# Second tile of the context's value sums: column-group matmuls by token in place of 128 multiply-adds on VectorE

## The chip, the cores and the metric

One core of a Trainium2 chip runs the whole program in one launch. The metric is the device time of one execution in microseconds; the median of several executions is compared. Engines are named as in the profile: PE is TensorE, DVE is VectorE, ACT is ScalarE, POOL is GpSimd and SP is SyncE, which issues most transfers.

## The reference, cut to what matters

The program is a transformer block with an MLP, then two layers of a second kind on 256 tokens `x`, beside a context `ctx` of 256 tokens which only the first of these layers updates. Each of them ends in an expert layer (`peer_ffn`): a token has 8 heads, each picks 16 of 16384 experts, so a token has 128 picks; `u` and `v` are rows of 1024 numbers.

```python
def chunk(hc):                      # 128 tokens
    ...                             # eid, gate: 128 tokens x 8 heads x 16 picks
    u = jnp.take(u_tab, eid, axis=0)
    act = jax.nn.gelu(jnp.einsum('chkd,cd->chk', u, hc)) * gate
    v = jnp.take(v_tab, eid, axis=0)
    return jnp.einsum('chk,chkd->cd', act, v)
```

The case is about the last line for the context: each token's output is the sum of its 128 rows of `v`, each times its own `act`. Everything is float32; the context's new state feeds the keys and values of the second layer's attention (`mla_kv`), and nothing else.

## The kernel before

**Two chains.** The main chain computes `x`: block 1, its MLP, then for each of the two layers a mixer and an expert layer in a dense form (every expert is multiplied for all tokens, and the gates are zero where it wasn't picked). Beside it runs the context's chain, `context` (L1502) and `context_peer` (L1514), as a Python generator: after each step of the main chain (one weight tile of 128x1024), `alongside` (L240) advances it by so many steps as the table `PACE` (L28) says for that stage. In the stage `out0` that is one step for each weight tile. A gather waits for the main chain's last weight tile (`behind`, L273), so the pace holds on the chip too. A scheduler then fixes each engine's order when the program is built.

**The main chain in `out0`** (`dense`, L1399, first expert layer): for each pair j of 128-expert columns, `scores` (L1387) makes 2 x 8 x 3 matmuls of 256 columns into `ps`, and `outputs` (L1418) 2 x 4 x 3 matmuls of 512 columns into `acc`. The factor 3 is `mm3` (L375, its three matmuls are L378 to L380): a float32 product is made from a high and a low half of each factor, `wh` by ACT (L363) and `wl` by DVE (L372) for every weight tile. `Gq` times the scores (`da`, L1412) and its halves `dh`, `dl` (L522, L523) are made once for each j. 64 j, four weight tiles each.

**After it** comes `mix1`, the second layer's mixer: first `add_tokens` (L1482) and the norm (L490 to L499), then projections of `w_in`, a convolution on DVE (L917), and its attention, which can't be started before the context's keys are ready (the word "keys" in `run`, L1606).

**The context's sums.** Tokens are in two tiles of 128. For a tile, `gather_acts` (L1225) gathers the rows of `u` and makes `act`, 128 tokens x 128 picks, and `gather_sum` (L1241) gathers the rows of `v`. Both use `fetch` (L1218): one indirect DMA of POOL's queue (L1220) brings 128 rows (512 KB) into one of the four buffers `ug`. The table `VSUM` (L41) chooses a form of the sum for each tile:

- 1, the second tile's: gather number k brings the k-th pick of all 128 tokens, one row for each partition (`eidi`); DVE multiplies it by that pick's `act`, a scalar for each partition, and adds it to `htok` (L1253; the first, L1251, only multiplies). At the end eight 128x128 transposes go through `gacc`, and eight DVE instructions (L1263) add them to the context.
- 0, the first tile's: a gather brings the 128 picks of one token (`eidT`, transposed on TensorE). TensorE sums over the partitions with the token's `act` as weights, so that one column of weights gives one token's sum. `Z` (tile `gz`, L1276) holds such columns spread over 32 columns, zero but for the token's own, and 32 tokens accumulate into 32 rows of PSUM. Two tokens (e) and two halves of the row (n) use four column groups of the array:

```python
for e in range(2):
    for n in range(2):
        c = 64 * n + 32 * e
        mul = nc.tensor.matmul(ga[c:c + 32, :], Z[:, e, m, :],
                               vt[e][0][:, n * 512:n * 512 + 512], start=(mm == 0),
                               stop=(mm == 31), skip_group_check=True, tile_position=(0, c))
        if e == 0:
            self.after(mul, vt[1][1])
```

The last two lines make the first of the four wait for both gathers. `ga` is the only buffer `gacc` of the context's chain. After 64 tokens (a half, q) ACT copies `ga` out (L1295), four transposes and eight DVE instructions (L1303) add it to the context, and `gacc` serves the second half. After the second tile's sum `keys_tile` (L931) makes the second half of the context's keys.

Of the kernel before, what the change touches and what calls it, by code (L numbers as in the profile page):

```python
# [37 lines left out]
TC = 16  # L38
GI = 8
VLOW = False  # L40
VSUM = (0, 1)  # L41
SHARE = ((0.24, 1.32), (0.24, 0.5))
MTS = (2, 2, 2)
DENSE = (2, 5)
# [152 lines left out]
class Net:  # L197
# [1043 lines left out]
    def gather_sum(self, s, x, gcol, tt, acc):  # L1241
# [3 lines left out]
        act = self.acts[tt]  # L1245
        if VSUM[tt]:
            ht = acc()
# [395 lines left out]
```

## Time and profile before

| | us |
|---|---|
| median of 3 runs | 3347.62 (3332.73 to 3351.87) |
| the profiled execution | 3326.9 |
| its span, first to last instruction | 3325.2 |
| TensorE busy in the span | 2956.7 (89%) |
| VectorE busy | 2472.0 (74%) |
| ScalarE busy | 1404.2 (42%) |
| GpSimd busy | 810.8 (24%) |

The profile is of one execution and gives each instruction its start, its length and the line that made it. Matmuls run pipelined, so their recorded lengths overlap: the time that one costs in a row of them is the distance between two starts. A matmul in full float32, such as L1288, leaves two records. "Idle before" is the time for which an engine stood still ahead of an instruction, with what ended it. The granted clock is a share of TensorE's full 2.4 GHz.

In the span, the first tile's sum runs from 969 to 1361 us, beside the first layer's mixer and routing. The second tile's runs from 1840 to 2302 us: beside `out0` until about 2165 us, and then beside the head of `mix1`.

### The profile page before, as it was taken

How to read it: one execution, taken by the hardware profiler on the slowest of the kernel's cores; microseconds unless marked ns; L12 is line 12 of the kernel's file. 1: busy time of each engine (PE TensorE's matmuls, PEld its weight loads, DVE VectorE, ACT ScalarE, POOL GpSimd, SP SyncE). 2: the span in 40 equal slices, each digit the busy share in tenths (PEclk: the TensorE clock that was granted, in tenths of full speed). 3: DMA queues.
4: the chain of work that ended last, by engine and by line, in shares of the span. 5: the costliest groups of instructions: out<-in, count | busy, mean ns of one | idle time of the engine just before them, and what ended most of it. 6: DMA issues, size and time to landing. Idle time of an engine off the chain costs nothing.

```text
span 3325.2 us, 52753 instructions
## 1 busy us (share of the span) xinstructions
PE 2956.7 (89%) x19879; PEld 2530.5 (76%) x19879; DVE 2472.0 (74%) x5129; ACT 1404.2 (42%) x1936; POOL 810.8 (24%) x565
## 2 busy tenths in 40 slices
PE   6989997888799899559999999988889899999998
PEld 4777786777676677348888888876669899888998
DVE  2645559999896579889888888968757998655555
ACT  2444553333334334234445444443434454544443
POOL 0000000444443234405442444511004433000000
PEclk9999988999799989669999999989989999999999
DMA  7777633899987579879998899966444489766664
GB/s 249 250 256 236 209 132 121 277 327 332 345 305 259 199 269 315 297 230 387 362 373 311 331 357 377 363 233 223 140 140 133 147 249 298 263 193 192 211 214 153
DMA packets 289327, 852.87 MB, mean 256 GB/s; under 512 B 25264, under 2 KB 91568, under 8 KB 284592
## 3 DMA queue, kind: packets, MB, share of 16 engines
q1 hardware_dynamic: 147888, 543.16, 47.8%
q0 software_dynamic: 73728, 268.47, 22.1%
q10 hardware_dynamic: 67456, 37.88, 3.8%
q8 instruction: 156, 2.56, 0.3%
q14 instruction: 99, 0.81, 0.1%
HBM read 814.80 MB, written 34.60 MB: 255 GB/s over the span
## 4 chain that ended last, share of the span: by engine, by line
PE 54%; DVE 18%; DMA 14%; issue 8%; ACT 3%; POOL 2%; SPq 0%; DVEq 0%; ACTq 0%; POOLq 0%
PE acc L379 7%; PE acc L380 6%; PE ps L380 6%; PE acc L378 6%; PE ps L378 6%; PE ps L379 6%; DVE wl L372 4%; DMA ug<-in_v_dram,eidT 3%; DMA w<-in_w_in_dram 3%; DMA ug<-in_u_dram,eidi 3%; DVE A L1373 2%; DVE ohB L1370 2%; DVE gz L1233 2%; DMA ug<-in_v_dram,eidi 2%; DMA w<-in_w_mod_dram 2%
## 5 line engine op out<-in xcount | busy, mean ns | idle before, releaser
L363 ACT ACTIVATE wh<-w 128x1024 fp32r<-128x1024 f32 (+1 forms) x818 | 850.5, 1045 | 1013.0 <-PE ps L379 276.3
L372 DVE TENSOR_TENSOR wl<-w,wh 128x1024 fp32r<-128x1024 f32 (+1 forms) x770 | 930.3, 1209 | 452.7 <-PE ps L380 114.8
L380 PE MATMUL ps<-hh,wl 128*128 128x256 f32 x2432 | 702.9, 290 | 30.4 <-DVE wl L372 30.2
L378 PE MATMUL ps<-hh,wh 128*128 128x256 f32 x2432 | 698.6, 288 | 26.8 <-ACT wh L363 14.6
L379 PE MATMUL ps<-hl,wh 128*128 128x256 f32 x2432 | 695.2, 286 | 3.0 <-DVE hl L523 2.9
L1220 POOL DMA_INDIRECT ug<-in_u_dram,eidi x256 | 346.8, 1355 | 1026.6 <-DVE rstd L479 562.5
L378 PEld LDWEIGHTS ps<-hh,wh 128*128 128x128 f32 x2432 | 470.5, 194 | 55.5 <-ACT wh L363 20.3
L380 PEld LDWEIGHTS ps<-hh,wl 128*128 128x128 f32 x2432 | 469.8, 193 | 56.1 <-DVE wl L372 42.4
L379 PEld LDWEIGHTS ps<-hl,wh 128*128 128x128 f32 x2432 | 470.3, 193 | 11.9 <-DVE hl L523 4.6
L379 PE MATMUL acc<-wl,dh 128*128 128x512 f32 x1024 | 407.2, 398 | 12.6 <-DVE wl L372 12.5
L378 PE MATMUL acc<-wh,dh 128*128 128x512 f32 x1024 | 403.4, 394 | 15.9 <-ACT dh L522 12.2
L380 PE MATMUL acc<-wh,dl 128*128 128x512 f32 x1024 | 400.8, 391 | 0.5 <-DVE dl L523 0.5
L1233 DVE SCALAR_TENSOR_TENSOR gz<-ug,htok 128x1024 bf16<-128x1024 f32 x256 | 310.5, 1219 | 22.3 <-DMA ug<-in_u_dram,eidi 22.0
L380 PE MATMUL pre<-hh,wl 128*128 128x256 f32 x896 | 261.8, 296 | 18.7 <-DVE wl L372 10.4
L1220 POOL DMA_INDIRECT ug<-in_v_dram,eidi x128 | 188.4, 1472 | 310.7 <-ACT wh L363 205.6
L379 PE MATMUL pre<-hl,wh 128*128 128x256 f32 x896 | 255.3, 287 | 0.0
L378 PE MATMUL pre<-hh,wh 128*128 128x256 f32 x896 | 254.8, 286 | 0.1
L379 PEld LDWEIGHTS acc<-wl,dh 128*128 128x128 f32 x1024 | 193.5, 189 | 63.4 <-DVE wl L372 28.0
L378 PEld LDWEIGHTS acc<-wh,dh 128*128 128x128 f32 x1024 | 193.6, 189 | 58.8 <-ACT dh L522 12.4
L372 POOL TENSOR_TENSOR wl<-w,wh 128x1024 fp32r<-128x1024 f32 x48 | 131.1, 2732 | 392.7 <-ACT wh L363 192.2
L380 PEld LDWEIGHTS acc<-wh,dl 128*128 128x128 f32 x1024 | 193.5, 189 | 39.8 <-DVE dl L523 1.2
L1220 POOL DMA_INDIRECT ug<-in_v_dram,eidT x128 | 143.2, 1118 | 258.8 <-PE gacc L1288 118.9
(510 smaller groups left out, 5108.1 us busy)
## 6 DMA issues: line engine op xcount, KB each, us to landing
w<-in_uT_dram SPq DMA_DIRECT2D x256, 512.0 KB, 4.6
w<-in_v_dram SPq DMA_DIRECT2D x256, 512.0 KB, 4.4
w<-in_w_in_dram SPq DMA_DIRECT2D x142, 512.0 KB, 4.6
w<-in_w_mod_dram SPq DMA_DIRECT2D x96, 512.0 KB, 4.9
w<-in_w_ff_dram SPq DMA_DIRECT2D x64, 512.0 KB, 5.9
G<-Gs ACTq DMA_DIRECT2D x32, 1024.0 KB, 7.3
Gq<-G SPq DMA_DIRECT2D x32, 1024.0 KB, 7.3
w<-in_w_ada_dram SPq DMA_DIRECT2D x48, 512.0 KB, 4.6
```

Of the source, the lines that this page charges most:

```text
L363: self.step = nc.scalar.activation(hi[:, :n], w[:, :n], AF.Copy)
L372: eng.tensor_tensor(lo[:, :n], w[:, :n], hi[:, :n].bitcast(F32), op=OP.subtract)
L378: mm(out, a[0], b[0], start=start, stop=False, skip_group_check=True)
L379: mm(out, a[0], b[1], start=False, stop=False, skip_group_check=True)
L380: mm(out, a[1], b[0], start=False, stop=stop, skip_group_check=True)
L1220: f = self.nc.gpsimd.indirect_dma_start(out=t, out_offset=None, in_=tab, in_offset=bass.IndirectOffsetOnAxis(ap=idx, axis=0))
L1233: nc.vector.scalar_tensor_tensor(j, ut, 1.0, ht, op0=OP.mult, op1=OP.mult, accum_out=sc[:, k:k + 1])
L1370: nc.vector.tensor_tensor(ohB, iov, over(iT[:, 1, ts]), op=OP.is_equal)
L1373: nc.vector.tensor_tensor(A2[:, i], ohA, over(gp[:, i, ts]), op=OP.mult)
```

## The change

One number in a table: the second tile's sum takes the first tile's form.

```diff
-VSUM = (0, 1)
+VSUM = (0, 0)
```

So for tokens 128 to 255 of the context L1251 to L1264 fall away, and L1266 to L1304 run, with 128 gathers by `eidT` where there were 128 by `eidi`, 256 matmuls L1288 in 64 groups of four, 16 products L1276, and the ends of two halves. The generator takes the same number of steps. What the engines' orders become is seen at four places.

DVE in the middle of `out0`, before: `wl` is the low half of a weight tile, `htok` the sum, `ug` a gathered tile, `da` and `dl` belong to the scores of a j.

```order
L372 TENSOR_TENSOR wl<-w,wh 128x1024
L1253 SCALAR_TENSOR_TENSOR htok<-ug,act,htok 128x1024
L1412 TENSOR_TENSOR da<-da,Gq 128x512
L372 TENSOR_TENSOR wl<-w,wh 128x1024
L1253 SCALAR_TENSOR_TENSOR htok<-ug,act,htok 128x1024
L523 TENSOR_TENSOR dl<-da,dh 128x512
L372 TENSOR_TENSOR wl<-w,wh 128x1024
L1253 SCALAR_TENSOR_TENSOR htok<-ug,act,htok 128x1024
L372 TENSOR_TENSOR wl<-w,wh 128x1024
L1253 SCALAR_TENSOR_TENSOR htok<-ug,act,htok 128x1024
```

DVE at the same place, of the change:

```order
L372 TENSOR_TENSOR wl<-w,wh 128x1024 x3
L1276 TENSOR_TENSOR gz<-eye_80,actT 128x256 x2
L1412 TENSOR_TENSOR da<-da,Gq 128x512
L523 TENSOR_TENSOR dl<-da,dh 128x512
L372 TENSOR_TENSOR wl<-w,wh 128x1024 x4
L1412 TENSOR_TENSOR da<-da,Gq 128x512
```

Where each `wl` had a multiply-add behind it, the `wl` now follow each other, with two products for `Z` every eight groups.

PE in the middle of `out0`, of the change: `acc` belongs to the outputs, `ps` to the scores, `gacc` to the context's sum.

```order
L378 MATMUL acc<-wh,dh 128x512
L379 MATMUL acc<-wl,dh 128x512
L380 MATMUL acc<-wh,dl 128x512
L1288 MATMUL gacc<-ug,gz 32x512 x4
L380 MATMUL ps<-hh,wl 128x256
L378 MATMUL ps<-hh,wh 128x256
L379 MATMUL ps<-hl,wh 128x256
```

In between the matmuls of the main chain stands a group of four; before, there was none here. From the start of the sum to the end of `out0` there are 53 such groups, two for each j; 11 more follow. From a group to the group after next, which uses its two buffers, TensorE mostly has four weight tiles of the main chain to do, at some places three or two. Behind `out0` the weight tile that releases a group's second gather stands at most two tiles ahead of the group.

PE at the end of `out0` and in the norm of `mix1`, before: `dout` is the output of the expert layer on its way back, the L490 sum the squares, L499 spreads the inverse root.

```order
L380 MATMUL acc<-wh,dl 128x512
L539 MATMUL ps<-cst,dout 128x128 x16
L490 MATMUL ps<-ones_74,mt 128x1 x8
L434 MATMUL pg<-w,ca_82 32x512 x4
L490 MATMUL ps<-ones_74,mt 128x1 x8
L499 MATMUL ps<-mt,ones_74 128x256
```

PE at the same place, of the change:

```order
L380 MATMUL acc<-wh,dl 128x512
L1288 MATMUL gacc<-ug,gz 32x512 x4
L539 MATMUL ps<-cst,dout 128x128 x8
L434 MATMUL pg<-w,ca_82 32x512 x4
L539 MATMUL ps<-cst,dout 128x128 x8
L1288 MATMUL gacc<-ug,gz 32x512 x4
L490 MATMUL ps<-ones_74,mt 128x1 x16
L1288 MATMUL gacc<-ug,gz 32x512 x4
L499 MATMUL ps<-mt,ones_74 128x256
```

Three groups have moved into this stretch, two of them in front of steps of the norm.

POOL, before, with all gathers of the program:

```order
L1220 DMA ug<-in_u_dram,eidi 128x1024 x128
L1220 DMA ug<-in_v_dram,eidT 128x1024 x128
L1220 DMA ug<-in_u_dram,eidi 128x1024 x128
L1220 DMA ug<-in_v_dram,eidi 128x1024 x128
L372 TENSOR_TENSOR wl<-w,wh 128x1024 x48
```

POOL, of the change:

```order
L1220 DMA ug<-in_u_dram,eidi 128x1024 x128
L1220 DMA ug<-in_v_dram,eidT 128x1024 x128
L1220 DMA ug<-in_u_dram,eidi 128x1024 x128
L1220 DMA ug<-in_v_dram,eidT 128x1024 x128
L372 TENSOR_TENSOR wl<-w,wh 128x1024 x48
```

Only the list of row numbers of the last 128 gathers is another.

## Rows read from the trace of the kernel before

**Rows 1.** Page, part 1: engine, busy us (share of the span), number of instructions

```profile
PE 2956.7 (89%) x19879; PEld 2530.5 (76%) x19879; DVE 2472.0 (74%) x5129; ACT 1404.2 (42%) x1936; POOL 810.8 (24%) x565
```

**Rows 2.** Stretch, its us; PE, PEld, DVE, ACT, POOL busy; granted clock; DMA share; GB/s

```profile
1843.00:2165.00 322.00, 309.54 (x1905) 273.24 (x1904) 286.35 (x294) 135.76 (x160) 158.87 (x105) 0.99 0.97 362
2165.00:2200.00 35.00, 24.01 (x134) 20.04 (x134) 23.55 (x64) 15.20 (x25) 2.67 (x3) 0.71 0.45 155
2200.00:2310.00 110.00, 97.22 (x705) 84.93 (x704) 88.80 (x176) 39.51 (x60) 22.24 (x18) 0.94 0.79 274
```

**Rows 3.** PE's waits, 1843 to 2165 us: for whom, us, times, longest; then to 2310

```profile
PE ps L380 <- DVE wl L372: 5.7, 5, 3.1
PE acc L379 <- DVE wl L372: 4.8, 3, 1.6
...
PE ps L380 <- DVE wl L372: 11.6, 10, 3.6
```

**Rows 4.** Timeline of PE in out0: start, length, operation

```profile
1910.13 0.28 PE L378 MATMUL ps<-hh,wh 128*128 128x256 f32 x1
...
1912.30 0.40 PE L378 MATMUL acc<-wh,dh 128*128 128x512 f32 x1
...
1916.86 0.39 PE L380 MATMUL acc<-wh,dl 128*128 128x512 f32 x1
```

**Rows 5.** Groups by line, 1850 to 2150 us: busy, mean ns, idle before and releasers

```profile
L1220 POOL DMA_INDIRECT ug<-in_v_dram,eidi x98 | 149.4, 1524 | 151.2 <-ACT wh L363 66.9 <-DVE htok L1253 38.7 <-DVE dl L523 19.6
L1253 DVE SCALAR_TENSOR_TENSOR htok<-ug,act,htok 128x1024 f32<-128x1024 f32 x97 | 124.1, 1280 | 10.2 <-DMA ug<-in_v_dram,eidi 10.2
...
L1412 DVE TENSOR_TENSOR da<-da,Gq 128x512 f32<-128x512 f32 x25 | 17.3, 690 | 14.6 <-ACT da L1397 14.5
```

**Rows 6.** DVE's groups, 1843 to 2310 us; then L1253's busy time in out0

```profile
L1253 DVE SCALAR_TENSOR_TENSOR htok<-ug,act,htok 128x1024 f32<-128x1024 f32 x127 | 162.5, 1279 | 27.6 <-DMA ug<-in_v_dram,eidi 27.5
L917 DVE SCALAR_TENSOR_TENSOR cacc<-up,cols,cacc 128x256 f32<-128x256 f32 x60 | 28.0, 480 | 0.0
...
1843.00:2165.00 322.00, 133.08 (x104) 0.99 0.97 362
```

**Rows 7.** Timeline of DVE in the norm at the head of mix1

```profile
2178.70 1.28 DVE L1253 SCALAR_TENSOR_TENSOR htok<-ug,act,htok 128x1024 f32<-128x1024 f32 x1 [1.09 <-DMA ug<-in_v_dram,eidi]
2181.34 0.16 DVE L493 TENSOR_SCALAR rstd<-ps 128x2 f32<-128x2 f32 x1 [1.36 <-PE ps L490]
```

**Rows 8.** Timeline of PE in the first tile's sum, full clock

```profile
1264.82 0.28 PE L380 MATMUL pre<-hh,wl 128*128 128x256 f32 x1
1265.03 1.07 PE L1288 MATMUL gacc<-ug,gz 128*32 128x512 f32 x8
1266.02 0.38 PE L380 MATMUL pre<-hh,wl 128*128 128x256 f32 x1
1266.24 0.28 PE L378 MATMUL pre<-hh,wh 128*128 128x256 f32 x1
```

**Rows 9.** A group after a wait, and the clock of its stretch (columns as rows 2)

```profile
1252.81 1.93 PE L1288 MATMUL gacc<-ug,gz 128*32 128x512 f32 x8 [2.55 <-DMA ug<-in_v_dram,eidT]
...
1252.80:1255.50 2.70, 2.69 (x12) 1.04 (x13) 2.18 (x16) 0.00 (x0) 0.50 (x1) 0.50 1.02 393
```

**Rows 10.** The small operations: durations in ns, minimum, median, maximum

```profile
L1276 DVE TENSOR_TENSOR gz<-eye,actT x16: 400/422/428, 968.4 to 1273.3; 128x256 f32<-128x256 bf16 x16
L1303 DVE SCALAR_TENSOR_TENSOR cT<-gacc,mod_b_mod,cT x16: 273/275/279, 1173.6 to 1364.3; 128x64 f32<-128x64 f32 x16
```

**Rows 11.** DMA issues, 1850 to 2150 us: count, median us from issue to landing

```profile
ug<-in_v_dram,eidi POOLq DMA_INDIRECT x98, 7.4
```

**Rows 12.** The first tile, 950 to 1352 us: PE's wait, POOL's group, landing

```profile
PE gacc L1288 <- DMA ug<-in_v_dram,eidT: 21.5, 17, 2.9
...
L1220 POOL DMA_INDIRECT ug<-in_v_dram,eidT x126 | 141.3, 1121 | 258.2 <-PE gacc L1288 118.9 <-ACT wh L363 67.1 <-issue 28.5
...
ug<-in_v_dram,eidT POOLq DMA_INDIRECT x126, 5.9
```

## The prediction

> **What bounds the kernel now.** I began with the page's busy line [rows 1]: TensorE is busy 89% of the span and VectorE 74%, an average over stages. The sum that changes runs from 1840 to 2302 us, so I asked for the busy time by stretch [rows 2]: 1843 to 2165 us (the gated sums of the first expert layer, "out0"), 2165 to 2200 us (the norm at the head of the second mixer) and 2200 to 2310 us (that mixer, "mix1"). In out0 TensorE is busy 309.5 of 322 us at a granted clock of 0.99, VectorE 286.4, and the DMA engines are at 97%. All three are near full, so the waits decide [rows 3]: of TensorE's 12.4 idle us in out0, 5.7 and 4.8 us ended with VectorE's low half of a weight tile (wl), the rest with ScalarE's high half (wh), none with a gather. TensorE bounds out0, and VectorE costs it little.
>
> How full that is shows in the starts of matmuls [rows 4]: from 1910.13 to 1912.30 us are 18 starts of 256 columns, 0.12 us each, and from there to 1916.86 us 20 starts of 512, 0.228 us each. A pair of expert columns (one j) has 48 of the first kind and 24 of the second: 48 x 0.12 + 24 x 0.228 = 11.2 us. By the row of L1412, the 25 j of 1850 to 2150 us [rows 5] took 300 / 25 = 12.0 us each. So 0.8 us in 12 are idle or hidden gaps, and nothing large that is added to TensorE fits into them.
>
> **What the change takes away.** VectorE loses one multiplication and 127 multiply-adds of 128x1024, 162.5 us, 133.1 of them in out0 and so 29.4 after it [rows 6]. None of it is directly on TensorE's path. What TensorE felt of it is the waits for wl, 5.7 + 4.8 in out0 and 11.6 - 5.7 = 5.9 after it, 16.4 us in all [rows 3]. A VectorE that has 133 of its 286 us less in out0 should come to nearly all of them in time: **-16.4 us**. Bounds: 0, if the late wl come from late weight tiles, and -28 if out0's hidden gaps go too (0.8 x 27 = 22 us there, 5.9 after). In the norm at 2178 us a multiply-add stands ahead of the first step of the inverse root (L493), but that step then still waited 1.36 us for TensorE [rows 7]: to drop it gives nothing there.
>
> **What it adds.** The 128 gathers, their queue on POOL and their pacing stay; they take their row numbers from the transposed list (order of POOL, in the section on the change). New are 64 groups of four matmuls, one for each two gathered tokens, on the engine that bounds. The first tile shows the price [rows 8]: a matmul of 256 columns starts at 1264.82, the group at 1265.03, and the next two at 1266.02 and 1266.24. From 1264.82 to 1266.24 are 1.42 us where two starts take 0.24 without it, so a group costs 1.18 us: 64 x 1.18 = **+75.5 us**. By the order of TensorE 53 groups stand in out0 (62.5 us) and 11 behind it (13 us). Of the 1.18 us, 0.09 lie ahead of the group and 0.10 behind it. The Trainium skill (TensorEngine Tiling (Array Packing), Key Properties) says that a change of tiling mode drains TensorE; by that rule these 0.19 us are the drain, which each group pays that stands alone, and the trace agrees that there is such a step. Without it the groups would cost 64 x 0.99 = 63 us, with it 75.5. Where the granted clock was 0.50 (1.2 GHz), right after TensorE had waited 2.55 us, a group took 1.93 us [rows 9]; that touches the groups in the norm, where the clock is 0.71 [rows 2], and adds some 2 us there, which I leave out. Could the groups hide? In out0 there are 12.4 us of idle time, and they belong to the waits just counted; in the norm and mix1 11.0 and 12.8 us [rows 2], scattered. So +75.5 stays, with +60 as its lower bound (11 groups hidden whole).
>
> Small additions: 16 products that spread the weights, 0.42 us each on VectorE (6.7 us); a transpose and copy of the activations; for each half of 64 tokens a copy, four transposes and eight short multiply-adds of 0.28 us [rows 10], where now eight of twice the columns end the sum. VectorE has room for all (133 us are freed), and the tail behind the last gather is as long as before within 2 us: 0.
>
> **The new wait.** Now a late gather holds VectorE, 27.5 us in all [rows 6]; afterwards it holds TensorE's queue, with all matmuls of the main path behind it. A group needs two gathers, and four buffers hold two groups; so a buffer comes free with a group, and the group after next uses it. In out0's order mostly four weight tiles stand between these, 4 x 2.8 = 11.2 us plus one group; against it stand two issues on POOL of 1.52 us and a landing of 7.4 us [rows 11], 10.4 us. That fits barely, and some groups stand only two or three tiles apart (5.6 to 8.3 us). The first tile, with the same buffers and the same groups, had 17 such waits, 21.5 us [rows 12], at a landing of 5.9 us and beside emptier DMA queues. Bounds: 0 (every gather in time) and +96 (1.5 us at each of 64 groups: the 10.4 us against three tiles and half a group). I take **+11**, between 0 and the first tile's 21.5, since TensorE's own slower pace (11.2 + 2 x 1.18 = 13.6 us for a j, not 12.0) spreads the same bytes over more time. The matmuls queued behind belong to the main path, and nobody else gets in between.
>
> **Sum:** -16.4 + 75.5 + 11 = +70 us. The profiled execution took 3326.9 us, so it would be 3397; the median of the three runs is 20.7 us above the profiled one, and the measured time is such a median: 3347.6 + 70 = **3418 us**.
>
> **The rivals.**
> *Gathers block TensorE.* If the round trip in out0 is longer than the tiles between a group and its refill, every group waits. For it: landings of 7.4 us in a stage at 97% DMA share, and mix1, where a gather's release stands only one or two tiles ahead of its group in the order. A long wait also brings the lower clock [rows 9]. Against it: VectorE waited only 10.2 us for 97 gathers of out0 [rows 5]. Half of the upper bound, +48 in place of +11: about 3455 us, up to 3503.
> *Gathers come sooner.* POOL's issue of a gather takes 1.52 us in out0 beside multiply-adds on VectorE, 1.12 us in the first tile's stretch [rows 5, 12]. If VectorE's work is what stretches it, two issues get 0.8 us shorter and the new waits vanish, while out0's hidden gaps go as well: 75.5 - 28 = +47, 3395 us. The Trainium skill (SBUF — State Buffer, Who interferes with whom) says that VectorE and GpSimd share a port pair which one instruction holds whole, and that VectorE instructions with two SBUF inputs contend with GpSimd's reads; by that rule this case is the likelier one, though the same section infers that writing descriptors needs only the write side. No run here separates the two yet.
> *No change.* The groups fall where TensorE would idle anyway. All 36 us of idle time in the three stretches of [rows 2] hold 36 of the 75.5; and mix1 ends sooner by the 28.0 us of its convolution on VectorE [rows 6], which starts earlier: +11.5, about 3359 us. The order speaks against it, since 53 groups stand where 12.4 us are idle.
> *Faster.* VectorE, not TensorE, paces out0: it is 89% busy, and TensorE's ends are modelled, so TensorE's busy share could flatter it. Then the 12.0 us of a j are VectorE's, and without 5.1 us of multiply-adds (four for a j) a j falls back to TensorE's 11.2 us plus what of two groups (2.4 us) does not overlap. It decides from the point where less than 0.8 us of these 2.4 lengthen a j; with a sixth (0.4 us) 12.0 becomes 11.6, over 27 j -11 us, and mix1's 12.8 idle us [rows 2] with its lighter VectorE make it -24: about 3324 us. Against it stand the 10.5 us of waits for wl in out0, far too few for an engine that sets the pace.
>
> **How the numbers follow.** Chances: forecast 0.58, gathers block 0.16, gathers sooner 0.14, no change 0.08, faster 0.04. All but the last two are slower. About 0.5%, 17 us, is what a measurement of this kernel can tell from no change: faster 0.04, same 0.08, slower 0.88. The range leaves out the fastest and most of the unchanged cases below (from +17, 3365 us) and above it ends within the upper half of the blocking case (+117, 3465 us).
>
> **What would show it right or wrong.** Right: in the profile after, out0 is about 55 us longer with TensorE still above 95% busy, a j takes some 13.7 us, the row of the group matmuls doubles its count, VectorE's busy time falls by about 155 us, and the waits of TensorE for wl shrink below 5 us. The new waits stand in TensorE's waits as "gacc <- DMA ug"; near 30 us in total (the first tile's 21.5 among them) they fit, near 70 the blocking rival holds. POOL's mean issue in out0 tells the third case: 1.5 us or near 1.0. The prediction is wrong if out0 gets no longer, which says that TensorE had room I did not see, or if a group of four costs clearly other than 1.18 us between 256- and 512-column matmuls.

## The result

| | median us | range | ratio to before, 95% interval |
|---|---|---|---|
| before, 6 runs | 3344.93 | 3332.73 to 3351.87 | |
| changed, 6 runs | 3364.61 | 3363.36 to 3369.87 | 1.0074 (1.0055 to 1.0093) |

The change makes the kernel slower by 0.74%, some 25 us (the two medians alone lie 20 us apart); the forecast was +70. The profiled execution of the changed kernel took 3363.4 us, its span is 3361.7.

Page, part 1, to be read against [rows 1]: TensorE gained 53 us and VectorE lost 137. The durations of VectorE's instructions fell by the 155 us that were worked out; its busy time fell by less, because recorded durations overlap in places.

```profile
PE 3010.0 (90%) x20392; PEld 2537.0 (75%) x20392; DVE 2335.3 (69%) x5026; ACT 1409.6 (42%) x1938; POOL 757.1 (23%) x565
```

Busy time by stretch, the stages of [rows 2] at their new places: out0, the norm, mix1 until the last group.

```profile
1839.00:2208.00 369.00, 364.55 (x2328) 282.53 (x2327) 177.27 (x215) 141.68 (x162) 107.53 (x104) 0.99 0.89 316
2208.00:2243.00 35.00, 28.73 (x196) 22.29 (x195) 20.01 (x61) 16.49 (x27) 4.70 (x5) 0.85 0.52 189
2243.00:2345.00 102.00, 97.61 (x751) 78.88 (x749) 74.94 (x208) 37.37 (x60) 19.18 (x16) 1.00 0.78 281
```

In out0 TensorE is now busy 364.55 of 369 us, and the DMA share fell from 0.97 to 0.89. In the norm and in mix1 TensorE has a higher granted clock than before, 0.85 against 0.71 and 1.00 against 0.94.

TensorE's waits in out0, and then from 2208 to 2345 us (for whom, us, times, longest), to be read against [rows 3]: the waits for wl are gone but for 0.4 us, the waits for gathers that came are 10.6 us.

```profile
PE gacc L1288 <- DMA ug<-in_v_dram,eidT: 4.5, 2, 2.6
...
PE gacc L1288 <- DMA ug<-in_v_dram,eidT: 6.1, 5, 1.8
...
PE ps L380 <- DVE wl L372: 0.4, 1, 0.4
```

A group in out0, in TensorE's timeline (start, length, operation): from 2000.70 to 2002.13 are 1.43 us where two starts take 0.24, so a group costs 1.19 us, as in the first tile [rows 8].

```profile
2000.70 0.28 PE L378 MATMUL ps<-hh,wh 128*128 128x256 f32 x1
2000.91 1.06 PE L1288 MATMUL gacc<-ug,gz 128*32 128x512 f32 x8
2001.91 0.38 PE L379 MATMUL ps<-hl,wh 128*128 128x256 f32 x1
2002.13 0.28 PE L380 MATMUL ps<-hh,wl 128*128 128x256 f32 x1
```

Groups by line, 1850 to 2200 us (busy, mean ns, idle before), against [rows 5]: POOL's issue of a gather takes 1.04 us, not 1.52.

```profile
L1220 POOL DMA_INDIRECT ug<-in_v_dram,eidT x100 | 103.8, 1038 | 252.0 <-PE gacc L1288 102.3 <-ACT wh L363 85.4 <-PE acc L380 19.1
L1288 PE MATMUL gacc<-ug,gz 128*32 128x512 f32 x408 | 54.4, 607 | 4.5 <-DMA ug<-in_v_dram,eidT 4.5
L1412 DVE TENSOR_TENSOR da<-da,Gq 128x512 f32<-128x512 f32 x25 | 17.3, 694 | 3.0 <-ACT da L1397 2.9
```

So price and number of the groups, the vanished waits and the new ones are all as forecast, and yet the profiled span grew by 36.5 us and the time by about 25. By the starts of marked instructions in the two traces: out0 (from the first L1412 on a `da` to the first L1488) is 47 us longer; the norm (to the first L378 of mix1) 3.3 us shorter, 19.4 in place of 22.7; mix1 (to the last L1063) 6.0 shorter, 182.5 in place of 188.5. The rest, ahead of out0 and behind mix1, is -4.2 and +3.1 us; behind mix1 two executions of one kernel differ by as much (next section). In out0 62.5 for its groups and 4.5 of new waits, less the 10.5 of vanished ones, were to give +56.5; behind it 13 + 6.1 - 5.9 were to give +13. So some 10 us are missing in out0, and 22 behind it.

### The profile page after: what moved, and what is told of

Read it like the earlier page. It is cut to its first block, busy times and chain, and to the rows that moved or that the text cites. A ratio compares the mean times of both kernels' runs of the same rounds, so it can differ in the third digit from the quotient of the medians.

```text
span 3361.7 us, 53689 instructions
## 1 busy us (share of the span) xinstructions
PE 3010.0 (90%) x20392; PEld 2537.0 (75%) x20392; DVE 2335.3 (69%) x5026; ACT 1409.6 (42%) x1938; POOL 757.1 (23%) x565
## 4 chain that ended last, share of the span: by engine, by line
PE 61%; DVE 16%; DMA 13%; issue 5%; ACT 3%; POOL 1%; SPq 0%; DVEq 0%; ACTq 0%; POOLq 0%
PE ps L380 7%; PE ps L378 7%; PE acc L379 7%; PE ps L379 7%; PE acc L380 7%; PE acc L378 7%; DMA ug<-in_v_dram,eidT 4%; DVE wl L372 3%; PE gacc L1288 3%; DMA ug<-in_u_dram,eidi 2%; DMA w<-in_w_in_dram 2%; DVE A L1373 2%; DVE ohB L1370 2%; DMA w<-in_w_mod_dram 2%; DVE gz L1233 2%
## 5 line engine op out<-in xcount | busy, mean ns | idle before, releaser
L378 PE MATMUL ps<-hh,wh 128*128 128x256 f32 x2432 | 700.4, 288 | 23.2 <-ACT wh L363 8.9
L378 PEld LDWEIGHTS ps<-hh,wh 128*128 128x128 f32 x2432 | 470.1, 193 | 65.4 <-issue 25.1
L1220 POOL DMA_INDIRECT ug<-in_v_dram,eidT x256 | 281.4, 1099 | 661.1 <-ACT wh L363 294.5
L378 PE MATMUL acc<-wh,dh 128*128 128x512 f32 x1024 | 402.5, 393 | 14.1 <-ACT dh L522 12.2
L1233 DVE SCALAR_TENSOR_TENSOR gz<-ug,htok 128x1024 bf16<-128x1024 f32 x256 | 310.4, 1218 | 19.4 <-DMA ug<-in_u_dram,eidi 19.2
L378 PE MATMUL pre<-hh,wh 128*128 128x256 f32 x896 | 255.4, 287 | 0.1
L378 PEld LDWEIGHTS acc<-wh,dh 128*128 128x128 f32 x1024 | 193.6, 189 | 57.0 <-ACT dh L522 12.5
L380 PEld LDWEIGHTS pre<-hh,wl 128*128 128x128 f32 x896 | 173.4, 195 | 38.4 <-DVE wl L372 15.0
```

What stands on the lines that cost most here:

```text
L378: mm(out, a[0], b[0], start=start, stop=False, skip_group_check=True)
L380: mm(out, a[1], b[0], start=False, stop=stop, skip_group_check=True)
L1220: f = self.nc.gpsimd.indirect_dma_start(out=t, out_offset=None, in_=tab, in_offset=bass.IndirectOffsetOnAxis(ap=idx, axis=0))
L1233: nc.vector.scalar_tensor_tensor(j, ut, 1.0, ht, op0=OP.mult, op1=OP.mult, accum_out=sc[:, k:k + 1])
```

## The experiments

Ratios are to the kernel before in runs beside each; times "x us above" are made from ratios, at 3340 us for the kernel before, whose medians there were 3336 to 3342. A ratio's interval is about 0.2% to either side, 7 us.

### The kernel before, once more

> The kernel before, unchanged, for a second profile. Its six times so far lie between 3332.7 and 3351.9 us, its one profile was of an execution of 3326.9 us, while the six times of the changed kernel lie within 6.5 us of each other. Theory A (the spread belongs to the multiply-adds on VectorE, which TensorE feels in some executions more than in others): the times spread over 15 to 25 us again, and a profile of a slower execution has its extra time in out0 and mix1, between 1840 and 2380 us. Rival: the spread lies elsewhere in the program, and the stretch from 1840 to 2380 us has the same length as in the first profile within 3 us.

Twelve times lie between 3333.6 and 3347.1 us (ratio 1.0002), and the second profile has a span of 3333.1 us, 7.9 above the first: 3.5 us of it in out0, 0.5 in the norm and mix1, 3.6 behind them. Neither theory holds: the difference is spread out, and the kernel without multiply-adds (below) spreads over 14 us too. What follows is smaller: my base, the median of three at 3347.6 us, was 5 to 11 us higher than every later median, and the profiled execution that carried the sum (3326.9 us) was quicker than every timed one of this kernel.

### What the multiply-adds cost by themselves

```diff
-                    nc.vector.scalar_tensor_tensor(ht, vt, act[:, k:k + 1], ht, op0=OP.mult, op1=OP.add)
+                    nc.vector.scalar_tensor_tensor(ht[:, 0:8], vt[:, 0:8], act[:, k:k + 1], ht[:, 0:8], op0=OP.mult, op1=OP.add)
```

> The kernel before, in which the 127 multiply-adds of the second tile read and write 8 of the 1024 columns only, so that the sums of the other columns are left out; the gathers, their order and their release by VectorE stay. It measures what the multiply-adds cost TensorE, by themselves. Theory A (they cost far more than the waits for wl that I counted: hidden gaps between matmuls in out0 and late steps in the norm and mix1 too): 35 to 55 us below the median of before, near 3300 us; out0 (sum's start to first dout) 16 to 22 us shorter than in the profile of before, norm and mix1 another 15 to 19. Theory B (the relief is the 16.4 us of waits for wl as forecast, and the groups cost less than 1.18 us each because part of them falls into idle time): 16 us below, near 3330. In both, POOL's mean issue of a gather falls to about 1.0 us if VectorE's work stretches it, and stays near 1.5 if it belongs to the kind of gather.

3316.8 us, ratio 0.9923 (0.9906 to 0.9940): 26 us below before, between the theories. POOL's issue stays at 1.43 us in out0. Out0 is 11 us shorter, mix1 3, and TensorE still waits for wl: 4.4 us in out0 and 9.6 behind it, though VectorE has next to nothing to do for the sum.

### Gathers that nothing reads

```diff
-                    nc.vector.scalar_tensor_tensor(ht, vt, act[:, k:k + 1], ht, op0=OP.mult, op1=OP.add)
+                    pass
```

> The kernel before, in which the second tile's 127 multiply-adds are left out whole, so that its sum is left out and nothing waits for a gather but the next gather into the same buffer. With e1_no_sum (3316.8 us), where VectorE still reads 8 columns of each gathered tile and so waits for it, this tells apart why TensorE still waited for wl there (4.4 us in out0, 9.6 in the norm and mix1). Theory A (a late gather holds VectorE, and the low halves queued behind it come late): those waits go, 8 to 14 us below e1_no_sum, 3303 to 3309. Theory B (the weight tiles themselves come late, with the DMA engines at 99% in out0): the waits stay, within 4 us of e1_no_sum.

3304.4 us, ratio 0.9891 (0.9868 to 0.9914), 11 us below the run just shown: theory A. TensorE's waits for wl in the norm and mix1, with 8 columns read:

```profile
PE ps L380 <- DVE wl L372: 9.6, 7, 2.6
```

and with nothing read:

```profile
PE ps L380 <- DVE wl L372: 1.0, 2, 0.8
PE ps L379 <- DVE wl L372: 0.8, 1, 0.8
```

An instruction of 0.2 us that stands at a late gather holds VectorE's queue, and the low halves behind it. The gain lies in mix1, 168.5 us long where it had 185.6; out0 is the same within 1 us. Gathers that nothing reads also start sooner, since no buffer waits for a reader; the run doesn't part these two.

### No gathers at all, and groups without gathers

```diff
-                vt, _ = self.fetch(A["v" + s], eidi[:, k:k + 1])
+                vt = vt if k else self.fetch(A["v" + s], eidi[:, k:k + 1])[0]
...
-                    nc.vector.scalar_tensor_tensor(ht, vt, act[:, k:k + 1], ht, op0=OP.mult, op1=OP.add)
+                    pass
```

> The kernel before without the second tile's sum and with only the first of its 128 gathers, so that the sum is left out. Against the gathers alone (3304.4 us). Theory A (what TensorE still lacked in out0, 11.65 us for a j in place of 11.2, are weight tiles that come late beside the gathers): out0 10 to 13 us shorter, a j near 11.2 us, and mix1 shorter by 5 to 15, near 3285 us. Theory B (it is TensorE's own): out0 as long, within 5 us.

```diff
-                        vt.append(self.fetch(A["v" + s], eidT[:, t:t + 1]))
+                        vt.append(held[e] if tt and len(held) > 1 else self.fetch(A["v" + s], eidT[:, t:t + 1]))
+                        held = held + [vt[e]] if len(held) < 2 else held
```

> The changed kernel with only the first two of the second tile's 128 gathers: all its 64 groups read these two tiles, so the sums are those of other rows. Groups without gathers; against the kernel without gathers and without sum. Theory A (a group costs its full time in out0, with nothing to fall into, and little behind it): 60 to 76 us above it, near 3350 us, out0 longer by 60 or more. Theory B (TensorE has room for them even so): under 50 us above it.

Without gathers 3280.7 us, ratio 0.9829 (0.9808 to 0.9849): 57 us below before. With the groups, 3363.9 us, ratio 1.0077 (1.0054 to 1.0099), 0.0248 x 3340 = 83 us above, more than theory A's 60 to 76. But these are not the groups of the changed kernel. All 64 stand in out0 (53 there), and the order often breaks them: here five matmuls, ten records, stand together and take 1993.33 to 1995.82 us, 2.03 us without the two starts around them, which is what eight take (2.05, groups twice, below).

```profile
1993.33 0.39 PE L378 MATMUL acc<-wh,dh 128*128 128x512 f32 x1
1993.65 1.90 PE L1289 MATMUL gacc<-ug,gz 128*32 128x512 f32 x10
1995.48 0.50 PE L379 MATMUL acc<-wl,dh 128*128 128x512 f32 x1
1995.82 0.40 PE L380 MATMUL acc<-wh,dl 128*128 128x512 f32 x1
```

Added up in this way over out0, 63 of its groups take 87 us, and the 52 that can be added up so in the changed kernel's out0 67, waits for gathers included. So the 83 us are the price of broken groups, and that the changed kernel with all its gathers (1.0074) is no slower than this one doesn't say that gathers are free beside groups. Busy time from 1880 to 2150 us, columns as [rows 2]; first the kernel before:

```profile
1880.00:2150.00 270.00, 260.13 (x1608) 230.11 (x1607) 241.38 (x239) 115.90 (x136) 135.72 (x89) 0.99 0.97 364
```

Gathers alone:

```profile
1880.00:2150.00 270.00, 265.83 (x1673) 236.00 (x1672) 143.13 (x146) 117.86 (x137) 128.08 (x92) 1.00 1.00 376
```

No gathers:

```profile
1880.00:2150.00 270.00, 270.00 (x1719) 245.77 (x1718) 152.88 (x166) 130.64 (x154) 0.00 (x0) 1.00 0.61 201
```

The changed kernel:

```profile
1880.00:2150.00 270.00, 265.55 (x1713) 203.74 (x1711) 124.16 (x133) 102.58 (x116) 86.09 (x82) 0.99 0.92 327
```

Groups alone:

```profile
1880.00:2150.00 270.00, 270.00 (x1678) 180.29 (x1676) 108.80 (x119) 88.07 (x100) 0.00 (x0) 1.00 0.45 144
```

With gathers alone the DMA engines are at 1.00, and TensorE is idle for 4 us though VectorE is idle for almost half the time: the weights come late beside the gathers. ScalarE, the first to use a weight tile, shows it. Its waits for weight tiles in the same 270 us (for whom, us, times, longest), in the kernel before:

```profile
ACT wh L363 <- DMA w<-in_v_dram: 13.2, 8, 2.3
...
ACT wh L363 <- DMA w<-in_uT_dram: 8.8, 8, 1.5
```

Gathers alone:

```profile
ACT wh L363 <- DMA w<-in_v_dram: 25.5, 17, 3.2
ACT wh L363 <- DMA w<-in_uT_dram: 17.3, 18, 1.6
```

The changed kernel:

```profile
ACT wh L363 <- DMA w<-in_v_dram: 3.2, 1, 3.2
...
ACT wh L363 <- DMA w<-in_uT_dram: 0.9, 1, 0.9
```

Without gathers there is one such wait, 2.5 us, and TensorE is never idle. The same in the length of a j, from the starts of L1412 in VectorE's timeline. Gathers alone, 16 j from the first to the last row, (2116.70 - 1928.32) / 16 = 11.77 us (12.0 before):

```profile
1928.32 0.69 DVE L1412 TENSOR_TENSOR da<-da,Gq 128x512 f32<-128x512 f32 x1 [2.23 <-ACT da L1397]
...
2116.70 0.69 DVE L1412 TENSOR_TENSOR da<-da,Gq 128x512 f32<-128x512 f32 x1 [2.23 <-ACT da L1397]
```

No gathers, 17 j, (2118.73 - 1927.65) / 17 = 11.24 us:

```profile
1927.65 0.69 DVE L1412 TENSOR_TENSOR da<-da,Gq 128x512 f32<-128x512 f32 x1 [0.17 <-ACT da L1397]
...
2118.73 0.69 DVE L1412 TENSOR_TENSOR da<-da,Gq 128x512 f32<-128x512 f32 x1 [0.17 <-ACT da L1397]
```

Against gathers alone, out0 is 9.7 us shorter without gathers and the norm 5, as in theory A; mix1, 168.7 us, is not shorter. In neither of the two kernels does anything pace the context's chain in out0, so the keys are made there too (kh at 1910 and 2187 us); the 21 us between no gathers and gathers alone hold this other order as well.

### Groups and multiply-adds together

```diff
+                        tt and _multiply_add(nc, ht, vt[e][0], act, t)
```

> The changed kernel, in which VectorE also makes its 128 multiply-adds of 128x1024 on the gathered tiles of the second sum, into a scratch tile that nothing reads. Groups and multiply-adds together; with the kernel before, the changed kernel and the one without either sum this makes a square of four. Theory A (the two costs add): 35 to 55 us above the changed kernel, near 3405 us. Theory B (relief of 16 us): near 3381. A third outcome, under 10 us above the changed kernel, would say that VectorE's multiply-adds cost nothing once TensorE's pace is slower. POOL's mean issue: 1.5 us if VectorE's work stretches it, 1.0 if the kind of gather decides.

3387.6 us, ratio 1.0141 (1.0125 to 1.0157): 22 us above the changed kernel, between the theories and nearer to B; the multiply-adds alone cost 26 above the kernel that only touches its tiles, so within the intervals the two costs add in the total. Not in out0, though: there the trace is 1.7 us longer than that of the changed kernel, the norm 6.7, mix1 13.6. POOL's issue of the same gathers from 1880 to 2150 us takes 1.33 us with the multiply-adds:

```profile
L1220 POOL DMA_INDIRECT ug<-in_v_dram,eidT x82 | 108.7, 1326 | 197.6 <-PE gacc L1288 66.2 <-DVE htok L1649 40.3 <-DVE wl L372 35.0
```

and 1.06 us without, in the changed kernel:

```profile
L1220 POOL DMA_INDIRECT ug<-in_v_dram,eidT x82 | 86.5, 1055 | 179.4 <-PE gacc L1288 87.4 <-ACT wh L363 42.5 <-PE acc L380 11.9
```

With gathers alone, by the other list of row numbers, it is 1.40 us:

```profile
L1220 POOL DMA_INDIRECT ug<-in_v_dram,eidi x92 | 128.5, 1397 | 141.0 <-ACT wh L363 101.7 <-DMA ug<-in_v_dram,eidi 24.2 <-issue 15.1
```

### Groups twice, and short groups

```diff
-                    for e in range(2):
+                    for e in list(range(2)) * (1 + tt):
```

> The changed kernel, in which every group of four matmuls of the second tile is issued twice in a row into the same sums, which doubles what they add. It measures what a group costs by itself. Theory A (a group costs its full time wherever it stands): 64 x 0.99 = 63 us above the changed kernel if the 0.19 us ahead of and behind a group are paid once for the pair, 64 x 1.18 = 75 if they are paid again, less some 5 to 10 us because waits for gathers shrink as TensorE gets slower: 3420 to 3435 us. Theory B (groups fall partly into idle time): 25 to 45 us above, near 3400.

Ratio 1.0262 (1.0239 to 1.0284), 63 us above the changed kernel, theory A: a second copy costs 63 / 64 = 0.98 us, and nothing of it hides. By the traces out0 is 45 us longer with its 53 copies, norm and mix1 together 15 with their 11. In the timeline a pair takes from 2003.93 to 2006.33 us, 2.05 us without the two starts around it (0.12 and 0.228):

```profile
2003.93 0.28 PE L380 MATMUL ps<-hh,wl 128*128 128x256 f32 x1
2004.14 1.92 PE L1288 MATMUL gacc<-ug,gz 128*32 128x512 f32 x16
2005.99 0.50 PE L378 MATMUL acc<-wh,dh 128*128 128x512 f32 x1
2006.33 0.40 PE L379 MATMUL acc<-wl,dh 128*128 128x512 f32 x1
```

So the second copy takes 0.86 us and the first 1.19. The Trainium skill (TensorEngine Tiling (Array Packing), Key Properties) says that a change of the tiling mode drains TensorE; the trace agrees that a group pays something that its copy doesn't, 0.33 us.

```diff
-                            mul = nc.tensor.matmul(ga[c:c + 32, :], Z[:, e, m, :],
-                                                   vt[e][0][:, n * 512:n * 512 + 512], start=(mm == 0),
+                            w = 8 if tt and mm > 0 else 512; mul = nc.tensor.matmul(ga[c:c + 32, 0:w], Z[:, e, m, :],
+                                                   vt[e][0][:, n * 512:n * 512 + w], start=(mm == 0),
```

> The changed kernel, in which all groups of the second tile but the first of each half read and write 8 of their 512 columns. Gathers, order, waits and the number of matmuls stay. Theory A (the price of a group is its columns, 0.95 of 1.19 us, and in out0 some 10 us of them lie in gaps that the late weight tiles leave): 35 to 45 us below the changed kernel, near 3325 us, and VectorE's low halves are waited for again in out0. Theory B (most of the price is the change to and from the narrow tiles, not the columns): under 20 us below, 3345 or more. Theory C (nothing is hidden): 60 us below, 3305.

3331.7 us, ratio 0.9976 (0.9958 to 0.9993), 33 us below the changed kernel: theory A but for 2 us. A short group costs 0.37 us (2007.76 to 2008.48, less 0.228 and 0.12):

```profile
2007.76 0.39 PE L380 MATMUL acc<-wh,dl 128*128 128x512 f32 x1
2008.08 0.25 PE L1288 MATMUL gacc<-ug,gz 128*32 128x8 f32 x8
2008.26 0.39 PE L378 MATMUL ps<-hh,wh 128*128 128x256 f32 x1
2008.48 0.28 PE L379 MATMUL ps<-hl,wh 128*128 128x256 f32 x1
```

Taken off were 62 x 0.82 = 51 us, and 33 came back. Unlike in what was expected, the order didn't stay: 45 groups stand in out0 and 19 behind it, where the changed kernel has 52 or 53 and 11 or 12. Out0 is 45 us shorter, some 37 for the columns of its 45 groups and the rest for the groups that left it; norm and mix1 are 8 us longer. So what didn't come back is lost behind out0, where more groups and gathers stand now. In out0 some waits for wl return, 2.8 us from 1880 to 2150 us.

The same edit for the 11 groups behind out0 alone (`tt and q and mm >= 21`):

> The changed kernel, in which the last 11 of the 64 groups, those behind out0, read and write 8 of their 512 columns, so that most of their sums is left out. It asks what the groups in the norm and in mix1 cost. In the traces norm and mix1 together took 211.2 us before, 208.0 without either sum and 201.9 with the 11 groups. Theory A (they stand where TensorE waits anyway): within 4 us of the changed kernel, 3361 to 3369 us. Theory A2 (they even help, since they keep TensorE's granted clock up in the norm): 2 to 6 us above it. Theory B (each costs its 1.19 us, as in the sum on record): 10 to 13 us below, 3352 to 3355.

3362.9 us, ratio 1.0070 (1.0046 to 1.0093): theory A, to take off their 11 x 0.82 = 9 us of columns gains nothing that can be measured. To add to these groups isn't free, though: the second copies behind out0 went with 15 us. A stretch of mix1, to the last gather (columns as [rows 2]), in the changed kernel:

```profile
2290.00:2333.00 43.00, 43.00 (x312) 33.65 (x311) 35.92 (x122) 15.00 (x22) 6.56 (x6) 1.00 0.69 243
```

and with the short tail:

```profile
2290.00:2332.00 42.00, 39.33 (x304) 32.54 (x303) 34.13 (x118) 14.12 (x21) 7.63 (x6) 0.97 0.76 261
```

With less work TensorE got a granted clock of 0.97 in place of 1.00, and idle time. That these take the gain isn't shown.

### Other paces

The number of the context's steps for a weight tile in out0, 1.0 in both kernels.

```diff
-        (1.16, 0.29), "pre0": (0.9, 1.4), "out0": (1.0, 2.8), "mix1": (0.7, 0.85)}
+        (1.16, 0.29), "pre0": (0.9, 1.4), "out0": (1.2, 2.8), "mix1": (0.7, 0.85)}
```

> The changed kernel with 1.2 steps of the context for a weight tile in out0 in place of 1.0: all 64 groups stand in out0 now, none behind it (53 and 11 before). Theory A (a group costs 1.19 us in out0 and nothing in the norm and mix1): 12 to 25 us above the changed kernel, 3377 to 3390 us, with out0 longer by 13 us and more waits for gathers, and norm and mix1 not shorter. Theory B (a group costs the same in both places): within 5 us of the changed kernel, norm and mix1 13 us shorter.

Ratio 1.0291, 72 us above the changed kernel: neither theory, because more moved than the groups. The last gather is issued at 2235 us, the keys are made inside out0 (kh at 2258 us), and in out0 TensorE waits 38.1 us for gathers, 16 times, where it waited 4.5.

Of the rivals this is the one in which gathers block TensorE, at a pace a fifth higher.

With 0.9, ten more groups stand behind out0; the second run is the same for the kernel before.

> The changed kernel with 0.9 steps of the context for a weight tile in out0 in place of 1.0: by the order of TensorE 43 groups stand in out0 and 21 behind it (53 and 11 in the changed kernel). Theory A (groups behind out0 are free): out0 12 us shorter, norm and mix1 as before, 8 to 14 us below the changed kernel, near 3355. Theory A2 (free for TensorE, but mix1 ends some 52 us after the context's keys, and those wait for more gathers): out0 12 us shorter, mix1 10 to 25 us longer, at or above the changed kernel. Theory B (a group costs the same anywhere): out0 12 us shorter, mix1 12 longer, within 4 us.

> The kernel before with the same pace of 0.9 in out0, as the control: the same gathers move behind out0, with multiply-adds on VectorE and no groups. Theory A: out0 gains little (2 to 4 us) and mix1 stays, within 5 us of the kernel before. Theory A2: mix1 10 to 25 us longer, 8 to 20 us above the kernel before.

Ratios 1.0141 and 1.0082: 22 us above the changed kernel, 27 above the one before. The direction of theory A2 in both: the last gather is issued 197 and 220 us behind the end of out0 (125 and 129 at pace 1.0), the keys come as late, and what follows mix1's last L1063 is 64 and 67 us longer: the second layer's attention waits. What a group behind out0 costs can't be read from them beyond this: moving groups there is no dearer than moving multiply-adds.

> The kernel before with 1.1 steps of the context for a weight tile in out0 in place of 1.0, so that some ten of the 20 gathers behind out0 stand in it. Theory A (what the sum costs in mix1 comes from its late gathers, and goes with them): mix1 10 us or more shorter, out0 up to 6 longer, 4 to 12 us below the kernel before, which would be faster than both kernels. Theory B (out0's DMA engines are full, and every gather moved there comes later): out0 longer by as much as mix1 gets shorter, or more, at or above the kernel before.

> As the run with 1.1, with 1.05: some five gathers move. Theory A: 2 to 6 us below the kernel before. Theory B: at or above it.

Both are the kernel before. With 1.1 the ratio is 1.0064 (1.0045 to 1.0082): in the traces out0 ends 72 us later, norm and mix1 are 26 us shorter and what follows 20, since the keys too are made in out0. Theory B. With 1.05 it is 0.9981 (0.9961 to 1.0001), no difference that this shows. The cost moves with the gathers.

### Later readers

```diff
-                vt, _ = self.fetch(A["v" + s], eidi[:, k:k + 1])
-                if k == 0:
+                if i < 128:
+                    late.append(self.fetch(A["v" + s], eidi[:, i:i + 1])[0])
+                ...
+                k, vt = i - 2, late.pop(0)
+                if k == 0:
```

> The kernel before, in which the multiply-add of a gathered tile is issued two steps after its gather and not right behind it, so that a late gather has two more weight tiles' time before VectorE stands at it. All work is done. The gathers without any reader took 11 us less than those that VectorE only touches, all of it in mix1. Theory A (a late gather holds VectorE and the low halves of the weights queued behind it): 8 to 14 us below the kernel before, near 3330 us, with mix1 shorter by about that and the waits for wl there gone. Theory B (the buffers are then freed two steps later, so that the gathers start later by as much and are as late as before): within 5 us of the kernel before.

> The changed kernel, in which in both tiles a group of four matmuls is issued one pair of gathers after its own pair. In the changed kernel TensorE waits 34.9 us for gathers in all, 21.5 of them at the first tile and some 13 at the second, of which 10.6 lie in out0, the norm and mix1. Theory A (they are waits for a landing, and one pair's time more covers them): 15 to 30 us below the changed kernel, 3335 to 3350. Theory B (four buffers hold two pairs, so a pair that is used later is refilled later, and the wait stays or grows): within 5 us of the changed kernel or above it.

> The kernel before with both: multiply-adds of the second tile two steps late, groups of the first tile one pair late. Theory A: 8 to 14 us from the second tile and some 10 to 18 of the first tile's 21.5 us, together 20 to 30 us below the kernel before, near 3316. Theory B: within 6 us of it.

> As the run with both, and the products with the gathered rows of u, which fix the activations, are issued two steps after their gathers too (VectorE stood 19.4 us before them for gathers). Theory A: another 3 to 10 us below the run with both, near 3310. Theory B: no difference to it beyond 4 us.

Ratios 0.9999, 1.0086 (1.0064 to 1.0108), 0.9993 and 1.0045 (1.0029 to 1.0060): theory B, no gain in any and a loss in the last. In the first, VectorE stands as long at its gathers between 1843 and 2310 us as before [rows 6]:

```profile
L1259 DVE SCALAR_TENSOR_TENSOR htok<-ug,act,htok 128x1024 f32<-128x1024 f32 x127 | 162.6, 1280 | 27.6 <-DMA ug<-in_v_dram,eidi 27.5
```

A reader that comes later frees its buffer later, and the next gather is late by as much. No version here that makes the whole sum beats the kernel before.

## Why the prediction was wrong

The ladder of ratios, in us against the kernel before, and beside it the lengths of the stages in the traces (of the kernel before, both of them):

| second tile's sum | us | out0 | norm | mix1 |
|---|---|---|---|---|
| no gathers, no sum | -57 | 568.2 | 17.4 | 168.7 |
| gathers alone | -36 | 577.9 | 22.3 | 168.5 |
| gathers, VectorE touches them | -26 | 578.3 | 22.4 | 185.6 |
| gathers and multiply-adds (before) | 0 | 589.4, 592.9 | 22.7, 23.5 | 188.5, 188.2 |
| groups alone, partly broken | +26 | 657.5 | 20.0 | 166.6 |
| gathers and groups (changed) | +25 | 636.3 | 19.4 | 182.5 |
| gathers, groups and multiply-adds | +47 | 638.0 | 26.1 | 196.1 |

- **What the change takes away** is the step that failed. I priced it by the waits for wl, 16.4 us, with 28 as the most. With the gathers kept and the multiply-adds gone the kernel is 36 us faster: some 26 for the multiply-adds and 11 for VectorE's standing at the gathers. By the traces 12 to 15 us of it lie in out0, where 10.5 were priced, and 20 in mix1, where it was 5.9 for all behind out0. Gathers that nothing reads also start sooner, and the 36 us hold that too.
- **What the change adds** has the right price and the wrong sum. A group costs 1.19 us and the new waits are 10.6, 86.5 in all by the forecast; but beside the gathers the groups with their waits cost 61 us (from -36 to +25). By the traces it is 58 in out0, where 62.5 + 4.5 were to come, and 11 behind it, where 13 + 6.1 were. So 25 = -36 + 61 stands where the forecast had 70 = -16.4 + 86.5.
- **Inside these steps** two things were wrong. "The 128 gathers, their queue on POOL and their pacing stay" is true of the code and was taken for a cost of nothing on either side; but the gathers cost out0 time because its weight tiles come late beside them (42.8 us of ScalarE's waits with gathers alone), and a TensorE that takes 14.0 us for a j, not 12.0, leaves the same bytes the time they need (4.1 us). And I read the relief from the waits that name wl, 10.5 of TensorE's 12.4 idle us in out0; the hidden 0.8 us of a j that I had worked out myself, and set aside as a bound, is the difference between 11.24 with neither gathers nor sum and 12.0 with both.
- **Out0**: +47 us measured against the first trace and +43 against the second, where 62.5 + 4.5 - 10.5 = 56.5 were to come. The 22 us of hidden gaps, my bound, are nearer than the 10.5 that I took.
- **Behind out0** lies the larger part of the miss: forecast 13 - 5.9 and the rest of the 11, measured -9. The stretch from the first L1488 to the last L1063 (columns as [rows 2]), before:

```profile
2166.20:2377.30 211.10, 176.54 (x1205) 152.63 (x1205) 159.34 (x410) 87.67 (x139) 24.91 (x20) 0.89 0.62 212
```

and after:

```profile
2208.80:2410.80 202.00, 178.12 (x1297) 146.73 (x1297) 136.13 (x387) 87.58 (x140) 23.16 (x21) 0.93 0.63 223
```

With the groups in it TensorE is busy 1.6 us longer and idle 10.7 us less, at a higher granted clock. How much of this is the clock isn't tested. What VectorE cost here is its standing at late gathers more than its arithmetic: with 8 columns read mix1 is 185.6 us long, with nothing read 168.5. In the norm I had a gain of 0; it got 3.3 us shorter with three groups in it. TensorE's timeline of the norm before: it stood idle for 2.79 us ahead of the sums L490 and 2.81 ahead of L499.

```profile
2173.23 2.71 PE L490 MATMUL ps<-ones,mt 128*128 128x1 f32 x16 [2.79 <-ACT mt L487]
2175.87 1.93 PE L434 MATMUL pg<-w,ca 128*32 128x512 f32 x8
2177.73 3.57 PE L490 MATMUL ps<-ones,mt 128*128 128x1 f32 x16
2184.11 1.22 PE L499 MATMUL ps<-mt,ones 128*128 128x256 f32 x2 [2.81 <-DVE mt L497]
```

After, the sums follow each other, with L434 ahead of them (at 2210.75 us, 1.07 us long), and a group fills most of the wait ahead of L499.

```profile
2215.73 4.99 PE L490 MATMUL ps<-ones,mt 128*128 128x1 f32 x32
2221.40 1.93 PE L1288 MATMUL gacc<-ug,gz 128*32 128x512 f32 x8 [0.68 <-DMA ug<-in_v_dram,eidT]
2223.53 1.22 PE L499 MATMUL ps<-mt,ones 128*128 128x256 f32 x2 [0.20 <-DVE mt L497]
```

The 32 sums took 2.71 + 3.57 us before and 4.99 after. That the groups help by keeping the clock up is not what the runs say: with the short tail, whose groups in the norm have 8 columns, its granted clock is 0.70 (0.68 before, 0.82 after), the sums take longer, and yet the norm is 18.5 us long.

```profile
2215.09 5.46 PE L490 MATMUL ps<-ones,mt 128*128 128x1 f32 x32
```

What that kernel shares with the changed one is the order. With gathers alone, where L434 stands between the sums as before, the norm takes 22.3 us. So the order is the likelier cause; no run changes it alone.

- **The rivals.** "Gathers come sooner" foresaw most of what came: POOL's issue near 1.0 us, no hidden gaps, few new waits. Its cause was only in part right: beside the same gathers the multiply-adds lengthen the issue from 1.06 to 1.33 us, but with gathers alone, by the list of before, it takes 1.40 us, so VectorE's work is not most of what makes 1.52. Whether the list of rows or the fuller DMA queues do, no run tells apart. And it knew nothing of the gathers' own cost. "Gathers block" holds at pace 1.2 and not at 1.0. "No change" had right that mix1 ends sooner (by 6 us, where it had 28), and the groups in out0 wrong. VectorE didn't pace out0, as "faster" has it: without the multiply-adds out0 is 11 to 15 us shorter, and with the groups it is 43 to 47 longer.
- **The base**: the median of three was 5 to 11 us too high, which is in the forecast time but not in its +70.
- **Open**: how the 21 us between no gathers and gathers alone divide between late weights and the order of the context's chain; what whole groups cost without gathers; how the gain behind out0 divides between idle time, clock and order.

## What to carry to other kernels

Price what a step costs now by taking it away, once with its transfers kept and once without them, not by the waits that name it: here they named 16 us of 36, and late weights beside full DMA engines spread over many small gaps. Where compute and DMA are both near full, work added to compute costs its full time, but it also gives transfers back theirs, so the net is smaller than the sum of instructions. Look at what an experiment's order became before its price is used: groups that a scheduler broke cost more than whole ones. A reader placed later doesn't cure a late transfer when its buffer is freed later too.

## What the runs showed of the hardware

- With gathers alone the DMA engines moved 376 GB/s in out0 at a share of 1.00. The Trainium skill (Perfetto Trace Analysis, Roofline) says that a core whose neighbour is idle can pull more than its 358 GB/s, up to what its 16 DMA engines carry; the trace agrees, and shows full engines at 105% of that figure.
- The Trainium skill (SBUF — State Buffer, Who interferes with whom) says that a VectorE instruction with two inputs in SBUF contends with GpSimd's reads. Beside multiply-adds the same gathers' issue took 1.33 us, without them 1.06, which fits it; the ports themselves show in no trace here. With gathers alone, by the other list of rows and at a DMA share of 1.00, it took 1.40, which that rule doesn't explain.
- A group of four matmuls of 8 columns takes 0.37 us between wide matmuls, one of 512 columns 1.19, and a second one right behind it 0.86. Five matmuls in a row take as long as eight (2.03 and 2.05 us): a broken group costs a whole one.
